# Recurrent gates in row halves of the array, and the first layer's mixing weights split by a converting DMA

## The chip, the cores and the metric

One core of a Trainium2 chip runs the whole program. The metric is the device time of one execution in microseconds (us), compared by the median of several runs. The engines are TensorE (PE, with its weight loads PEld), VectorE (DVE), ScalarE (ACT), GpSimd (POOL) and SyncE (SP, which only issues DMAs).

## The reference, cut to what matters

An encoder of two layers on 512 tokens of 1024 channels, float32. Each layer is a mixing part (half of it attention in a window, half a recurrence in both directions) and a gated MLP with a convolution. The change touches the recurrence: 512 channels in 8 blocks of 64; per direction two gates, each a 64x64 matrix per block.

```python
def rg_lru(x, w_gate, b_gate, lam, reverse):
    xb = x.reshape(bsz, s, N_LRU_BLOCKS, LRU_BLOCK)
    g = jnp.einsum("bsnc,gncd->gbsnd", xb, w_gate).reshape(2, bsz, s, D_LRU)
    g = g + b_gate[:, None, None, :]
    r_gate = jax.nn.sigmoid(g[0]); i_gate = jax.nn.sigmoid(g[1])
    log_a = -LRU_C * r_gate * jax.nn.softplus(-lam)
    a = jnp.exp(log_a)
    u = jnp.sqrt(-jnp.expm1(2.0 * log_a)) * (i_gate * x)
    return linear_scan(a, u, reverse)
...
rec = (rec_f + rec_b) * jax.nn.gelu(gate, approximate=True)
```

## The kernel before, in words

Activations lie channels by tokens, in tiles of 128 partitions x 512 tokens. To reach float32 accuracy each operand of a big product is split in two float32r parts, a leading one (hi) and a trailing one (lo = value - hi), and each product is three TensorE products (`mm3`, L234 to L237: hi x hi, hi x lo, lo x hi).

Weights come in an order fixed by `weight_plan` (L57), in blocks of up to 1024 columns. `chunk` (L223) hands out the next block and keeps the preparation ahead: `load_to` (L162) issues the load on SP's queue into one of 2 `raw` buffers (L177), `split_to` (L182) lets ScalarE copy to `hi` (L197) and VectorE subtract to `lo` (L198), with 4 buffers each. The second layer's mixing blocks are split during the first layer's MLP by `split_later` (L204), kept in DRAM, and loaded back ready (L172).

The order of the mixing part is written out by hand in `MIX` (L44): q, k, v and g are the four column products of the input projection, in halves a and b of 12 products each; c the convolution of a recurrence tile; t0 to t3 the gates of a tile of 128 channels; S, T and P the scores, transposes and products of a head; u turns the values and copies them into `edge` on GpSimd (L603); e multiplies the recurrence by its gate branch (L624). Between these, a planner puts each engine's instructions in an order of its own, by priority and estimated times, and that order is fixed: every engine and every queue then works in order.

`lru_gates` (L521) runs twice per tile: t_a for the forward, t_b for the backward direction. Each call makes two gates of 128x128 weights, in which the two 64x64 blocks stand on the diagonal and the rest is zero; six products of 512 columns. ScalarE takes tanh from the PSUM bank (L535) and makes the decay, VectorE the input term (L542, L543, L549), then one scan per direction (L552, L555) and the sum of both into `fb` (L557). The products' banks come from a pool of three, `ps_mm` (L124).

## Time and profile before

| what | us |
|---|---|
| median of 3 runs | 1210.29 (1209.95 to 1210.47) |
| the profiled execution's own time | 1209.74 |
| span of the profiled execution | 1208.0 |

The profile is of one execution. The span goes from its first to its last instruction; busy times are of that span. A matmul record covers the whole passage through the array, so records overlap, and the distance from one start to the next is what a product costs in a stream. An arrow in a wait leads to what ended it.

### The profile page before, as it was taken

How to read it: one execution, taken by the hardware profiler on the slowest of the kernel's cores; microseconds unless marked ns; L12 is line 12 of the kernel's file. 1: busy time of each engine (PE TensorE's matmuls, PEld its weight loads, DVE VectorE, ACT ScalarE, POOL GpSimd, SP SyncE). 2: the span in 40 equal slices, each digit the busy share in tenths (PEclk: the TensorE clock that was granted, in tenths of full speed). 3: DMA queues.
4: the chain of work that ended last, by engine and by line, in shares of the span. 5: the costliest groups of instructions: out<-in, count | busy, mean ns of one | idle time of the engine just before them, and what ended most of it. 6: DMA issues, size and time to landing. Idle time of an engine off the chain costs nothing.

```text
span 1208.0 us, 14574 instructions
## 1 busy us (share of the span) xinstructions
PE 1192.5 (99%) x5566; PEld 996.3 (82%) x5566; DVE 757.0 (63%) x1237; ACT 502.3 (42%) x741; POOL 95.1 (8%) x166
## 2 busy tenths in 40 slices
PE   9999999999999999999999999999999999999996
PEld 8878888888888888888888888888888888888886
DVE  7899867866634567653728868486555345565353
ACT  6777744434321334332406778353233212333220
POOL 1010010123210123200000000000000000000000
PEclk9999999999999999999999999999999999999998
DMA  7222213367652467633255542233233232323222
GB/s 239 69 87 86 90 41 123 123 223 247 214 168 90 151 218 243 210 117 105 88 174 164 164 141 71 65 111 102 90 102 95 97 104 88 105 87 105 92 66 70
DMA packets 51061, 151.85 MB, mean 126 GB/s; under 512 B 6448, under 2 KB 9648, under 8 KB 50992
## 3 DMA queue, kind: packets, MB, share of 16 engines
q1 hardware_dynamic: 42208, 122.61, 31.3%
q0 software_dynamic: 8640, 28.32, 7.2%
q8 instruction: 43, 0.70, 0.3%
q14 instruction: 26, 0.21, 0.1%
q10 hardware_dynamic: 144, 0.00, 0.0%
HBM read 129.93 MB, written 20.97 MB: 125 GB/s over the span
## 4 chain that ended last, share of the span: by engine, by line
PE 94%; DVE 4%; issue 1%; POOL 0%; DMA 0%; ACT 0%; POOLq 0%; DVEq 0%; SPq 0%; ACTq 0%
PE dn L237 7%; PE dn L235 7%; PE dn L236 7%; PE pl L237 7%; PE pa L237 7%; PE pa L235 7%; PE pl L235 7%; PE pl L236 7%; PE pa L236 7%; PE out L237 2%; PE out L235 2%; PE out L236 2%; PE xr L235 1%; PE up L235 1%; PE vps L237 1%; PE vps L235 1%
## 5 line engine op out<-in xcount | busy, mean ns | idle before, releaser
L197 ACT ACTIVATE hi<-raw 128x1024 fp32r<-128x1024 f32 (+1 forms) x189 | 197.5, 1046 | 399.3 <-PE dn L236 160.5
L198 DVE TENSOR_TENSOR lo<-raw,hi 128x1024 fp32r<-128x1024 f32 (+1 forms) x189 | 228.0, 1206 | 133.5 <-ACT hi L197 132.4
L805 DVE TENSOR_TENSOR ua<-pa,g_ffn_rb 128x512 f32<-128x512 f32 x44 | 30.4, 692 | 113.7 <-PE pa L237 113.7
L813 ACT ACTIVATE uc<-uc,cols 128x512 f32<-128x512 f32 x48 | 34.8, 725 | 117.4 <-DVE uc L811 117.4
L814 DVE TENSOR_TENSOR uc<-pl,uc 128x512 f32<-128x512 f32 x44 | 30.3, 689 | 44.7 <-PE pl L237 43.9
L782 DVE TENSOR_TENSOR dns<-dn,g_ffn_rb 128x512 f32<-128x512 f32 x30 | 20.5, 689 | 29.4 <-PE dn L237 29.4
L811 DVE SCALAR_TENSOR_TENSOR uc<-ua,cols,uc 128x511 f32<-128x511 f32 x48 | 36.0, 750 | 1.5
L809 DVE SCALAR_TENSOR_TENSOR uc<-ua,cols,uc 128x511 f32<-128x511 f32 x48 | 35.8, 745 | 0.1
L220 POOL DMA_DIRECT2D kept<-lhi x36 | 19.6, 544 | 177.3 <-ACT lhi L214 175.3
L215 DVE TENSOR_TENSOR llo<-lraw,lhi 128x512 fp32r<-128x512 f32 x36 | 24.7, 688 | 10.7 <-ACT lhi L214 10.7
L453 POOL TENSOR_TENSOR fin_r<-fin_ms,expo 128x2 f32<-128x2 f32 x2 | 1.4, 697 | 377.7 <-DVE fin_ms L451 377.7
L669 ACT ACTIVATE prob<-prob,mx 128x192 f32<-128x192 f32 (+1 forms) x64 | 27.4, 430 | 1.1 <-DVE mx L667 0.9
L603 POOL CAST edge<-vh 64x384 fp32r<-64x384 f32 x16 | 8.9, 558 | 236.4 <-ACT vh L598 235.9
L235 PE MATMUL out<-atth,hi 128*128 128x512 f32 x64 | 25.6, 401 | 0.0
L237 PE MATMUL out<-atth,lo 128*128 128x512 f32 x64 | 25.3, 395 | 0.0
L236 PE MATMUL out<-attl,hi 128*128 128x512 f32 x64 | 25.2, 393 | 0.0
L808 DVE TENSOR_SCALAR uc<-ua,cols 128x512 f32<-128x512 f32 x48 | 23.4, 488 | 1.6
L220 POOL DMA_DIRECT2D kept<-llo x36 | 19.6, 544 | 50.5 <-DVE llo L215 47.7
L214 ACT ACTIVATE lhi<-lraw 128x512 fp32r<-128x512 f32 x36 | 22.1, 616 | 0.0
L654 PEld LDWEIGHTS s<-k,q_pair 128*128 128x128 f32 x128 | 20.8, 190 | 1.2
L654 PE MATMUL s<-k,q_pair 128*128 128x192 f32 (+1 forms) x128 | 21.7, 313 | 0.0
L783 DVE TENSOR_TENSOR x<-x,dns 128x512 f32<-128x512 f32 x30 | 20.1, 688 | 0.4
(931 smaller groups left out, 3616.0 us busy)
## 6 DMA issues: line engine op xcount, KB each, us to landing
raw<-in_w SPq DMA_DIRECT2D x183, 512.0 KB, 3.5
lraw<-in_w POOLq DMA_DIRECT2D x36, 256.0 KB, 4.4
kept<-lhi POOLq DMA_DIRECT2D x36, 256.0 KB, 2.5
kept<-llo POOLq DMA_DIRECT2D x36, 256.0 KB, 3.0
hi<-kept SPq DMA_DIRECT2D x36, 256.0 KB, 2.9
lo<-kept SPq DMA_DIRECT2D x36, 256.0 KB, 4.2
x<-in_x SPq DMA_DIRECT2D x8, 256.0 KB, 5.3
out_y<-out SPq DMA_DIRECT2D x8, 256.0 KB, 2.3
```

The lines of the kernel that those rows point to most:

```text
L197: nc.scalar.activation(hi[:, sl], raw[:, sl], AF.Copy)
L198: nc.vector.tensor_tensor(out=lo[:, sl], in0=raw[:, sl], in1=f32(hi[:, sl]), op=ALU.subtract)
L220: nc.gpsimd.dma_start(d, f32(parts[h][n]))
L235: nc.tensor.matmul(ps, a[0], b[0], start=start, stop=False)
L236: nc.tensor.matmul(ps, a[0], b[1], start=False, stop=False)
L237: nc.tensor.matmul(ps, a[1], b[0], start=False, stop=stop)
L654: nc.tensor.matmul(ps[:, o:o + ROWS * w], q_pair[:, b], kt[:, kc0 // 8:(kc0 + w) // 8], start=True, stop=True)
L805: nc.vector.tensor_tensor(out=ua, in0=pa, in1=rbf[0], op=ALU.mult)
L809: nc.vector.scalar_tensor_tensor(out=c[:, 1:], in0=ua[:, :T - 1], scalar=w[0], in1=c[:, 1:], op0=ALU.mult, op1=ALU.add)
L811: nc.vector.scalar_tensor_tensor(out=c[:, :T - 1], in0=ua[:, 1:], scalar=w[2], in1=c[:, :T - 1], op0=ALU.mult, op1=ALU.add)
L813: nc.scalar.activation(c, c, AF.Gelu_apprx_tanh, bias=col("conv_ffn_b", j, l))
L814: nc.vector.tensor_tensor(out=c, in0=pl_, in1=c, op=ALU.mult)
```

## The change

The gates of both directions of a tile now stand in one 128x128 block per gate: block row half s holds, in its columns, the forward matrix of sub-block s in the same half and the backward one in the other half. A product of one half of the rows (64 partitions in, 128 out) gives both directions of one sub-block. So a call makes one gate for both directions: three products for each row half, each half in a PSUM bank of its own. The first call (t_a) makes the decay gate of both directions, the second (t_b) the input gate, the root and the scans. The backward direction then has its two halves of 64 channels in swapped places: `xc_sw`, a copy of the convolved tile with halves swapped, is made by two DMAs on GpSimd's queue, and the backward scan is put onto `fb` by two DMAs that swap back and add. ScalarE's tanh works on 64 partitions at a time. A gate block has 256 columns in place of 512.

In the first layer's mixing part the blocks q, k, v, g and the gates, 20 in all, get `hi` by a DMA on GpSimd's queue that converts float32 to float32r as it writes, and `raw` by a second load on SP's queue; VectorE subtracts. A load of these goes at most three blocks ahead of the one in use, a subtraction two. The host lays out gate weights, biases and decays to match.

```diff
@@ weight_plan
-                plan.append(("gate", l, [(int(step[1]), dg) for dg in range(4)]))
+                plan.append(("gate", l, [(int(step[1]), g) for g in range(2)]))
@@ encoder
+    def segments(i):
+        return [slice(a, min(a + 512, width(i))) for a in range(0, width(i), 512)]
...
-    def is_kept(i):
-        w, l, bs = plan[i]
-        return l == 1 and (w == "gate" or w == "w_in" and bs[0][1] != 12)
+    def by_dma(i):
+        w, _, bs = plan[i]
+        return w == "gate" or w == "w_in" and bs[0][1] != 12
@@ load_to
-            if is_kept(i):
+            if by_dma(i):
                 if i > state["use"] + 3:
                     return
                 highs[i] = p_hi.tile([P, 1024], F32R, tag="hi", name=f"hi{i}")
...
+                if i in kept:
+                    lows[i] = p_lo.tile([P, 1024], F32R, tag="lo", name=f"lo{i}")
+                    for n, t in enumerate((highs[i], lows[i])):
+                        for h, sl in enumerate(segments(i)):
+                            nc.sync.dma_start(f32(t[:, sl]), kept[i][n, h])
+                else:
+                    ws = slice(0, width(i))
+                    nc.gpsimd.dma_start(highs[i][:, ws], w_d[i][:, ws])
+                    raws[i] = p_raw.tile([P, 1024], F32, tag="raw", name=f"raw{i}")
+                    nc.sync.dma_start(raws[i][:, ws], w_d[i][:, ws])
@@ split_to
-            if is_kept(i) and i > state["use"] + 2:
+            if by_dma(i) and i > state["use"] + 2:
                 return
...
+            if i in highs:
+                hi = highs.pop(i)
+                lo = p_lo.tile([P, 1024], F32R, tag="lo", name=f"lo{i}")
+                ws = slice(0, width(i))
+                nc.vector.tensor_tensor(out=lo[:, ws], in0=raws.pop(i)[:, ws], in1=f32(hi[:, ws]), op=ALU.subtract)
+                halves[i] = (hi, lo)
+                state["split"] += 1
+                continue
...
-    later = [i for i in range(len(plan)) if is_kept(i)]
+    later = [i for i in range(len(plan)) if by_dma(i) and plan[i][1] == 1]
@@ convolve
             xcs[t] = plain_split(p_h, "h", c, f"xcs{l}_{t}")
+            xc_sw[t] = big(p_h, "h", f"xsw{l}_{t}")
+            swapped(xc_sw[t], c)
@@ layer
+        rows_of = (slice(0, 64), slice(64, P))
+        def swapped(dst, src, **kw):
+            for n in range(2):
+                nc.gpsimd.dma_start(dst[rows_of[n]], src[rows_of[1 - n]], **kw)
@@ lru_gates (new)
+            def products(g, out):
+                ps = [psum(ps_o if n and g and not o_ps[0] else ps_mm, f"gp{l}{t}{g}{n}") for n in range(2)]
+                w = blk(gate["c"], g)
+                for a, b in ((0, 0), (0, 1), (1, 0)):
+                    for n, rows in enumerate(rows_of):
+                        nc.tensor.matmul(ps[n], w[a][rows], xcs[t][b][rows], start=a + b == 0, stop=a == 1)
+                for n in range(2):
+                    for d in range(2):
+                        i = ((l * 2 + d) * 2 + g) * 4 + t
+                        rows = rows_of[n ^ d]
+                        with urgent():
+                            nc.scalar.activation(out[d][rows], ps[n][rows], AF.Tanh, scale=0.5, bias=half_b[rows, i:i + 1])
...
+            if 0 in gs:
+                products(0, ws)
...
+            if 1 in gs:
+                ti = [big(p_t, "t", f"ti{l}{t}{d}") for d in range(2)]
+                products(1, ti)
+                nc.scalar.activation(both, both, AF.Sqrt, scale=0.25)
+                for d, (a, w, u) in enumerate(zip(gate["a"], ws, ti)):
+                    nc.vector.scalar_tensor_tensor(out=u, in0=u, scalar=1.0, in1=xc_sw[t] if d else xc[t],
+                                                   op0=ALU.add, op1=ALU.mult)
+                    nc.vector.tensor_tensor(out=u, in0=u, in1=w, op=ALU.mult)
...
+                        nc.vector.tensor_tensor_scan(out=w[:, ::-1], data0=a[:, ::-1], data1=u[:, ::-1], initial=0.0,
                                                      op0=ALU.mult, op1=ALU.add)
-                    nc.vector.tensor_tensor(out=fb[t], in0=fb[t], in1=w, op=ALU.add)
+                        swapped(fb[t], w, accum_op=ALU.add)
@@ lay_out
-                gate[:, :, 2 * d + g, 64 * s:64 * s + 64, 64 * s:64 * s + 64] = a["lru_w"][:, d, g, s::2]
+            o = 64 * (s ^ d)
+            gate[:, :, :, 64 * s:64 * s + 64, o:o + 64] = a["lru_w"][:, d, :, s::2].transpose(0, 2, 1, 3, 4)
```

## Rows read from the trace of the kernel before

**Rows 1.** the page, part 1: busy time, share of the span, instructions

```profile
PE 1192.5 (99%) x5566; PEld 996.3 (82%) x5566; DVE 757.0 (63%) x1237; ACT 502.3 (42%) x741; POOL 95.1 (8%) x166
...
core 0: 1208.0 us, clock 0.996
```

**Rows 2.** busy time by stage; TensorE, weight loads, VectorE, ScalarE, GpSimd, clock, DMA share, GB/s

```profile
0.00:37.00 37.00, 35.95 (x163) 30.50 (x164) 29.98 (x64) 21.45 (x31) 5.31 (x17) 1.00 0.62 209
37.00:170.00 133.00, 130.80 (x671) 110.39 (x670) 115.61 (x251) 101.28 (x181) 10.80 (x16) 1.00 0.26 81
70.00:102.00 32.00, 31.88 (x167) 27.18 (x166) 29.52 (x66) 25.81 (x46) 2.43 (x4) 1.00 0.25 80
636.00:763.00 127.00, 126.16 (x654) 107.38 (x653) 98.74 (x234) 87.17 (x163) 9.70 (x16) 1.00 0.42 133
```

**Rows 3.** timeline of TensorE, first gate call: start us, duration us, operation

```profile
36.93 0.39 PE L235 MATMUL gp<-xcs_0h,hi 128*128 128x512 f32 x1
37.15 0.39 PE L236 MATMUL gp<-xcs_0l,hi 128*128 128x512 f32 x1
...
38.29 0.39 PE L235 MATMUL kps<-xg_g_mix_4h,hi 128*128 128x512 f32 x1
```

**Rows 4.** the tile gp: duration ns min/median/max of weight loads and products

```profile
L235 PEld LDWEIGHTS gp<-xcs_0h,hi x8: 187/188/188, 36.7 to 636.1; 128*128 128x128 f32 x8
L235 PE MATMUL gp<-xcs_0h,hi x8: 389/389/389, 36.9 to 636.3; 128*128 128x512 f32 x8
```

**Rows 5.** timeline of TensorE, attention products of 128 columns

```profile
75.05 0.22 PE L235 MATMUL o<-pt,edge 128*128 128x128 f32 x1
75.11 0.28 PE L236 MATMUL o<-pt,edge 128*128 128x128 f32 x1
```

**Rows 6.** timeline of TensorE, from the scores back to f32r products

```profile
50.16 0.48 PE L235 MATMUL gate<-xg_g_mix_0h,hi 128*128 128x512 f32 x1
50.48 0.40 PE L236 MATMUL gate<-xg_g_mix_0l,hi 128*128 128x512 f32 x1
```

**Rows 7.** groups of ScalarE by shape, 30 to 170 us: busy us, mean ns

```profile
L197 ACT ACTIVATE hi<-raw 128x1024 fp32r<-128x1024 f32 x17 | 17.9, 1051 | 9.6 <-DMA raw<-in_w 6.1 <-PE gate L236 3.5
...
L535 ACT ACTIVATE w<-gp,half_b 128x512 f32<-128x512 f32 x8 | 5.4, 677 | 9.5 <-PE gp L237 9.5
...
L197 ACT ACTIVATE hi<-raw 128x512 fp32r<-128x512 f32 x3 | 1.9, 617 | 0.0
```

**Rows 8.** groups of VectorE by shape, 30 to 170 us

```profile
L198 DVE TENSOR_TENSOR lo<-raw,hi 128x1024 fp32r<-128x1024 f32 x18 | 22.3, 1238 | 2.2 <-ACT hi L197 1.9
...
L567 DVE TENSOR_TENSOR q_pair<-qps,g_mix_rb 64x512 f32<-64x512 f32 x8 | 5.5, 687 | 0.5 <-PE qps L237 0.4
...
L557 DVE TENSOR_TENSOR fb<-fb,w 128x512 f32<-128x512 f32 x4 | 2.7, 686 | 0.1
```

**Rows 9.** groups of GpSimd, the whole span

```profile
L211 POOL DMA_DIRECT2D lraw<-in_w x36 | 20.0, 558 | 1.2 <-DVE h_11l L352 1.2
```

**Rows 10.** DMA issues: KB each, median us to landing

```profile
raw<-in_w SPq DMA_DIRECT2D x183, 512.0 KB, 3.5
lraw<-in_w POOLq DMA_DIRECT2D x36, 256.0 KB, 4.4
```

**Rows 11.** waits, 37 to 170 us: us in total, times, longest

```profile
ACT hi L197 <- DMA raw<-in_w: 6.1, 3, 3.1
...
PE o L237 <- POOL edge L603: 1.0, 2, 0.5
```

**Rows 12.** timeline of VectorE, end of the scans of gate tile 2

```profile
120.01 1.20 DVE L555 TENSOR_TENSOR_SCAN w<-a,ti 128x512 f32<-128x512 f32 x1
121.24 0.69 DVE L557 TENSOR_TENSOR fb<-fb,w 128x512 f32<-128x512 f32 x1
...
127.94 0.68 DVE L624 TENSOR_TENSOR fb<-fb,z 128x512 f32<-128x512 f32 x1
```

**Rows 13.** timeline of GpSimd, the same stretch

```profile
122.61 1.12 POOL L603 CAST edge<-vh 64x384 fp32r<-64x384 f32 x2 [27.74 <-ACT vh L598]
```

More of the change, by code (lines that the diff above doesn't have):

```diff
@@ L151, in pieces @@
     def pieces(i):
[L152 removed]
+        return (slice(0, 1024),) if i else (slice(0, 512), slice(512, 1024))
     def width(i):
         return P * len(plan[i][2])
[L157 to L160 removed]
+    def segments(i):
[3 more added lines that the diff above has]
+        return w == "gate" or w == "w_in" and bs[0][1] != 12
     def load_to(n):
@@ L168, in load_to @@
                 highs[i] = p_hi.tile([P, 1024], F32R, tag="hi", name=f"hi{i}")
-                lows[i] = p_lo.tile([P, 1024], F32R, tag="lo", name=f"lo{i}")
-                for n, t in enumerate((highs[i], lows[i])):
-                    for h in range(width(i) // 512):
-                        nc.sync.dma_start(f32(t[:, 512 * h:512 * h + 512]), kept[i][n, h])
+                if i in kept:
[8 more added lines that the diff above has]
+                    nc.sync.dma_start(raws[i][:, ws], w_d[i][:, ws])
                 state["load"] += 1
@@ L208, in split_later @@
         parts = []
-        for h in range(width(i) // 512):
-            raw = p_t.tile([P, 512], F32, tag="t", name=f"lraw{i}{h}")
-            nc.gpsimd.dma_start(raw, w_d[i][:, 512 * h:512 * h + 512])
-            hi = p_fb.tile([P, 512], F32R, tag="fb", name=f"lhi{i}{h}")
-            lo = p_fb.tile([P, 512], F32R, tag="fb", name=f"llo{i}{h}")
+        for h, sl in enumerate(segments(i)):
+            n = sl.stop - sl.start
+            raw = p_t.tile([P, n], F32, tag="t", name=f"lraw{i}{h}")
+            nc.gpsimd.dma_start(raw, w_d[i][:, sl])
+            hi = p_fb.tile([P, n], F32R, tag="fb", name=f"lhi{i}{h}")
+            lo = p_fb.tile([P, n], F32R, tag="fb", name=f"llo{i}{h}")
             nc.scalar.activation(hi, raw, AF.Copy)
@@ L217, in split_later @@
         for n in range(2):
-            for h in range(width(i) // 512):
-                d = p_kept.tile([P, 512], F32, tag=f"kept{i}{n}{h}", name=f"kept{i}{n}{h}")
+            for h, sl in enumerate(segments(i)):
+                d = p_kept.tile([P, sl.stop - sl.start], F32, tag=f"kept{i}{n}{h}", name=f"kept{i}{n}{h}")
                 nc.gpsimd.dma_start(d, f32(parts[h][n]))
@@ L497, in layer @@
             prepare_decay()
-        xr, xc, xcs = [], [None] * 4, [None] * 4
+        xr, xc, xcs, xc_sw = [], [None] * 4, [None] * 4, [None] * 4
         for t in range(4):
@@ L513, in convolve @@
             xcs[t] = plain_split(p_h, "h", c, f"xcs{l}_{t}")
+            xc_sw[t] = big(p_h, "h", f"xsw{l}_{t}")
+            swapped(xc_sw[t], c)
         fb = [None] * 4
[L518 removed]
+        gate = {}
         o_ps, att_t = [None], [None]
[L521 to L557 removed]
@@ L885, in lay_out @@
         blocks[n] = w.reshape(L, w.shape[1] // P, P, w.shape[2] // P, P).transpose(0, 1, 3, 2, 4)
-    gate = np.zeros((L, 4, 4, P, P), np.float32)
+    gate = np.empty((L, 4, 2, P, P), np.float32)
     for s in range(2):
         for d in range(2):
-            for g in range(2):
-                gate[:, :, 2 * d + g, 64 * s:64 * s + 64, 64 * s:64 * s + 64] = a["lru_w"][:, d, g, s::2]
+            o = 64 * (s ^ d)
+            gate[:, :, :, 64 * s:64 * s + 64, o:o + 64] = a["lru_w"][:, d, :, s::2].transpose(0, 2, 1, 3, 4)
     blocks["gate"] = gate
@@ L907, in lay_out @@
             put(COLS[n, l], a[n][l])
-    for n in ("lru_b", "lru_lam", "g_final"):
-        put(COLS[n], a[n])
+    lru = {}
+    for n in ("lru_b", "lru_lam"):
+        v = a[n].reshape(L, 2, -1, 2, 64).copy()
+        v[:, 1] = v[:, 1, :, ::-1]
+        lru[n] = v
+    for n, v in (("lru_b", lru["lru_b"]), ("lru_lam", lru["lru_lam"]), ("g_final", a["g_final"])):
+        put(COLS[n], v)
     rel = a["rel_bias"]
```

58 lines of the change are left out of this document (20 added, 38 removed).

## The prediction

> **What bounds the kernel now.** I read the busy times first: TensorE is busy 1192.5 of the 1208.0 us of the span, at a granted clock of 0.996, which is the 2.4 GHz level [rows 1]. So the end is set by TensorE's stream of products, and an edit counts only as far as it takes time from that stream or opens a hole in it. Then the table by stage, for the two stretches in which the gates are computed. In the first layer's mixing TensorE is busy 130.80 of 133 us, VectorE 115.61, ScalarE 101.28, GpSimd 10.80; in the second layer's 126.16 of 127, 98.74, 87.17 and 9.70 [rows 2]. The holes are 2.2 and 0.8 us. In one full turn of the first layer (70 to 102 us) VectorE is busy 29.52 of 32: it follows close behind TensorE, and is the engine that would stop it next.
>
> The profiled execution took 1209.74 us, 1.74 around the span; the median of the runs is 1210.29, so 0.55 is added to a sum made on the trace. A measurement of this kernel tells about 0.2% (2.4 us) from no change.
>
> **Part 1: the gate products in row halves.** Six products of one call run from 36.93 to 38.29 us, so 0.227 us each, end to start [rows 3]. There are 12 in each of 4 tiles and 2 layers, 96, so 21.8 us of TensorE. After it there are again 96 products and 96 weight loads, of 64 rows each, in 48 pairs whose halves use different rows of the array and different PSUM banks. If a pair runs side by side it takes 0.227 us, the whole 48 x 0.227 = 10.9, and 10.9 us leave the stream. If the halves run one after the other, nothing leaves it.
>
> Do the loads of weights allow a pair? A load lasts 0.187 us [rows 4], but a product of 128 columns starts at 75.05 and the next, with weights of its own, at 75.11 [rows 5]: loads follow each other every 0.06 us, and two of them fit into 0.227. I take the pair at 0.227.
>
> What a change between 128 and 64 rows costs no row shows. It happens on entering and on leaving each of 16 calls, 32 times. Lower bound 0, since between products of one kind there is no gap. Upper bound: the engine empties each time, which is how far a product's record outlasts the start of its successor, 0.389 - 0.227 = 0.162 [rows 3, 4], plus 0.06 at the end of each call for the half that started a load later: 32 x 0.162 + 16 x 0.06 = 6.2. The nearest row is the switch from the f32 scores to f32r products, where the first product takes 50.48 - 50.16 = 0.32 in place of 0.227, 0.09 more [rows 6]. I take 32 x 0.09 = 2.9, since that is also a change of how the array works.
>
> Part 1 on TensorE: -10.9 + 2.9 = -8.0.
>
> **The evacuation.** Tanh over a tile becomes two half tiles of 64 partitions. VectorE's 64x512 operation takes 0.687, like its 128x512 ones [rows 8], so a half costs ScalarE what a whole did, 0.677 [rows 7] (lower bound half of it). That is 4 more per tile, +2.7 us, 10.8 per layer. In the second layer ScalarE goes to 98 of about 123 us, a share of 0.80, where the first layer now has 0.76: cover enough. The banks: a call's two banks are both free after four halves, 2.7 us, in place of 1.4; between the two calls of a tile stand 12 key products, 12 x 0.227 = 2.7. That just fits; were it gone, each second call would wait up to 1.3 us.
>
> **Part 2: the first layer's mixing weights.** 16 blocks of 1024 columns and 4 of the gates lose their ScalarE pass: 16 x 1.051 + 4 x 0.617 = 19.3 us [rows 7], more than the 10.8 that the halves add. This is off the path; I count it at nothing. VectorE keeps its subtraction, 1.238 each [rows 8]; the gates' falls from 512 to 256 columns, worth 0 to 0.34 each. VectorE also loses the four additions of the two scans per layer, 4 x 0.686 = 2.7 [rows 8]. Per turn VectorE falls by about 1.0 from 29.5 and TensorE by about 1.0 from 32: it stays as close behind as it was.
>
> GpSimd's queue gets 20 converting loads and, in two layers, 32 copies of half tiles. An issue takes 0.558 [rows 9], so 36 in the first layer are 20 us beside its 10.80 of 133: hidden. What can stand behind one are the edge copies, for which TensorE already waits 1.0 us in that stretch [rows 11]. In the turn shown the second scan ends at 121.21; two adding copies issue until 122.3; the next edge copies start at 122.61 [rows 12, 13]. They fit by 0.3. The adding copies must land before the multiplication by the gate branch at 127.94 [rows 12]; at the 4.4 us of the slowest comparable load [rows 10] they land at 126.7. Hidden by 1.2 us; if it slips, VectorE stands there and everything behind it.
>
> SP's queue keeps 20 loads, of the same blocks; the bytes double for these 20, some 8.5 MB over 133 us, at a DMA share that stands at 0.26 [rows 2]: hidden. At the start, where the share is 0.62, one converting load of 0.5 MB at 209 GB/s could push the others by 2.5 us; TensorE had no hole there beyond its first microsecond [rows 2], and I take 0 of 0 to 2.5.
>
> What can't be read is how long a converting load takes. Lower bound: a plain load of such a block, 3.5 us; from above the GpSimd load of half the size, 4.4, and twice that, 8.8 [rows 10]. A block's tile comes free, and the load goes, four uses ahead; the subtraction stands two uses ahead, so between them one block's products, 24 x 0.227 = 5.4 us, and less around a gate block. I take 5 us, near the GpSimd load, and the wait as mostly covered.
>
> **The sum.** -8.0 from the gates. Holes: TensorE comes to each wait about 1 us earlier while what it waits for is about as late, so the 3.0 us of holes may grow; ScalarE's relief pulls the other way. Bounds -3.0 and +3.0, I take +0.5. Together -7.5: 1209.74 - 7.5 = 1202.2, and 1202.8 against the median.
>
> **The rivals.**
> *The halves don't overlap* (the change does not do what it says). Each half product then takes its own 0.227, 96 of them, the 2.9 of mode changes come on top, and the kernel is at 1213. For it: the trace has no product of fewer than 128 rows. Against it: weights and products already overlap freely. It decides from the point at which a pair takes over 0.39 us.
> *The engine empties at each change.* Then the upper bound of 6.2 holds in place of 2.9: -10.9 + 6.2 + 0.5 = -4.2, 1206.1. For it: between unlike products the rows do show lost time [rows 6]. Against it: those rows lose half as much. The Trainium skill (TensorEngine Tiling (Array Packing), Key Properties) says that changing the tiling mode drains the engine; no run here shows it yet.
> *The weight loads bind.* If a pair must wait for two loads end to end, 2 x 0.187 = 0.374, a pair saves 0.454 - 0.374 = 0.08, 3.8 in all, 2.9 of it eaten: 1209.4. Against it stand the loads at 0.06. The Trainium skill (TensorE: Matmul & The Clock Gate, Part 3) has loads overlap running products only when the row groups differ; the trace does not agree, since loads of all rows run beside products of all rows here at 0.227.
> *VectorE stands at the conversion.* Its queue is in order, and the subtraction now waits for two loads. Before, ScalarE stood for the raw load three times, 6.1 us in all, 2.0 each [rows 11], with time to spare. VectorE has 133 - 115.6 = 17 us free in that stretch; 20 waits use it up from 0.85 us each. At 2.0 each, 40 - 17 = 23 us come through: 1226, slower. For it: a landing that is unknown, a queue that is 0.92 full in the turn. Against it: the lead above. A milder form, in which TensorE gets 3 to 7 us of holes, gives 1206 to 1210.
>
> **How the numbers follow.** Overlapping halves and covered loads 0.52 (1198.4 to 1206; the lower end is -10.9 with 1 us of the holes gone); the engine empties 0.12; the milder stand of VectorE 0.12, half of it beyond 1207.9; loads bind 0.08; no overlap 0.09; VectorE stands in full 0.07. So faster by over 0.2% (under 1207.9) 0.52 + 0.12 + 0.06 = 0.70; within 0.06 + 0.08 = 0.14; slower (over 1212.7) 0.09 + 0.07 = 0.16. The range from 1198 to 1211 holds the first four, 0.84.
>
> **What would show it.** Right: gate products whose second half starts some 0.06 us after the first and pairs 0.227 apart, so 5 us fewer in each layer's mixing; the first product after a call late by about 0.09; ScalarE's share in the first layer down by some 8 us; GpSimd's share up by 20; holes of TensorE near 3 us. Wrong: halves 0.227 apart; the subtractions or the gate branch's multiplication waiting on DMA for more than 17 us in all; TensorE waiting for edge copies or for ScalarE's halves for more than 3 us.

## The result, and the profile after

The changed kernel takes 1218.28 us (median, 1215.70 to 1219.41, 4 runs) against 1210.12 beside it: a ratio of 1.0066, 95% interval 1.0054 to 1.0077. It is **slower by 8.2 us**, where 1202.8 was forecast and the range ended at 1211. The profiled execution took 1215.70, 2.6 under the median.

The page, part 1, the span, and the busy time by stage, each stage taken from the same work as in [rows 2] (columns as there):

```profile
PE 1193.5 (98%) x5566; PEld 989.1 (81%) x5566; DVE 747.1 (62%) x1229; ACT 503.6 (41%) x753; POOL 126.9 (10%) x218
...
core 0: 1213.9 us, clock 0.994
...
38.00:174.00 136.00, 130.32 (x669) 106.37 (x668) 109.49 (x247) 98.82 (x182) 28.15 (x45) 0.99 0.49 143
640.00:771.00 131.00, 126.18 (x653) 104.27 (x650) 96.14 (x231) 97.19 (x179) 19.25 (x30) 0.99 0.46 137
```

TensorE does not set the time alone any more: it stands for 5.7 us of the first stretch and 4.8 of the second, against 2.2 and 0.8 before. It is as busy as before although the calls save 2.3 us in each, since products under a lower clock take longer (below). ScalarE has lost only 2.5 us in the first layer, where the prediction named some 8: four wide conversions of other weights stand in the same stretch and stayed. In the second layer it has gained 10.

**The products are faster, by less than forecast.** Timeline of TensorE around the first gate call, which answers to [rows 3] ("x2" is a pair):

```profile
37.48 0.39 PE L255 MATMUL kps<-xg_g_mix_3h,lo 128*128 128x512 f32 x1
37.80 0.50 PE L562 MATMUL gp<-xcs_0h,hi 64*128 64x512 f32 x2
38.14 0.40 PE L562 MATMUL gp<-xcs_0l,hi 64*128 64x512 f32 x2
38.37 0.40 PE L562 MATMUL gp<-xcs_0h,lo 64*128 64x512 f32 x2
38.70 0.50 PE L253 MATMUL kps<-xg_g_mix_4h,hi 128*128 128x512 f32 x1
39.04 0.40 PE L254 MATMUL kps<-xg_g_mix_4l,hi 128*128 128x512 f32 x1
```

The halves of a pair start together and run side by side: three pairs take 0.90 us, six products took 1.36. But the first step into the call and the one behind it take 0.32 and 0.34, and inside it only the middle pair takes 0.23. From the last product before the call to the second one after it 1.56 us pass, before it was 8 x 0.227 = 1.82. Of the 16 calls, ten save 0.26 like this one and six, which come after a 128-column product, 0.34: 10 x 0.26 + 6 x 0.34 = 4.6 us in all, not 8.0.

**The two long holes.** In both layers the first product that reads `vl` comes late. VectorE, GpSimd's queue and TensorE in the first layer:

```profile
64.49 1.23 DVE L205 TENSOR_TENSOR lo<-raw,hi 128x1024 fp32r<-128x1024 f32 x1 [1.82 <-DMA hi<-in_w]
65.63 0.69 DVE L370 TENSOR_TENSOR xcs_1l<-xc,xcs_1h 128x512 fp32r<-128x512 f32 x1
66.23 0.68 DVE L637 TENSOR_TENSOR vl<-vtp,vh 128x512 fp32r<-128x512 f32 x1
...
57.94 1.73 POOL L545 DMA_DIRECT2D fb<-w  x2 [7.82 <-ACT pt L733]
59.32 0.95 POOL L179 DMA_DIRECT2D hi<-in_w  x1
...
66.97 0.39 PE L255 MATMUL o<-pt,vl 128*128 128x256 f32 x1 [2.63 <-DVE vl L637]
```

The subtraction waits for a converting load; the load was issued behind two adding DMAs on the same queue; `vl` stands behind the subtraction, and TensorE waits 2.63 us for `vl`. The second layer:

```profile
662.63 0.69 DVE L662 TENSOR_TENSOR fb<-fb,z 128x512 f32<-128x512 f32 x1 [3.04 <-DMA fb<-w]
663.25 0.69 DVE L370 TENSOR_TENSOR xcs_1l<-xc,xcs_1h 128x512 fp32r<-128x512 f32 x1
663.85 0.68 DVE L637 TENSOR_TENSOR vl<-vtp,vh 128x512 fp32r<-128x512 f32 x1
...
664.58 0.39 PE L255 MATMUL o<-pt,vl 128*128 128x256 f32 x1 [2.51 <-DVE vl L637]
```

Here it is the multiplication by the gate branch that waits, for the adding DMA. In the kernel before, the same two products start without a wait:

```profile
66.35 0.30 PE L237 MATMUL o<-pt,vl 128*128 128x256 f32 x1
...
657.37 0.39 PE L237 MATMUL o<-pt,vl 128*128 128x256 f32 x1
```

Behind each hole TensorE's products of 512 columns come 0.43 us apart instead of 0.227 for a while:

```profile
69.89 0.63 PE L255 MATMUL kps<-xg_g_mix_0h,lo 128*128 128x512 f32 x1
70.32 0.63 PE L253 MATMUL kps<-xg_g_mix_1h,hi 128*128 128x512 f32 x1
...
68.50:71.70 3.20, 3.20 (x12) 2.62 (x10) 3.14 (x7) 0.49 (x1) 0.59 (x2) 0.50 0.74 197
```

The last line is the table by stage for that stretch: the granted clock is 0.50, the 1.2 GHz level; TensorE had stood 2.63 us and then worked for 1.5 us at 1.00 before it fell. Seven products from 68.89 to 71.99 take 3.10 where 7 x 0.227 = 1.59 would do, so this hole costs 1.5 us more than its length.

The waits of VectorE behind this (37 to 176 and 632 to 772 us), the DMAs' landing, and ScalarE's halves (30 to 174 us), which answer to [rows 11], [rows 10] and [rows 7]:

```profile
DVE lo L205 <- DMA hi<-in_w: 15.1, 7, 3.2
...
DVE fb L662 <- DMA fb<-w: 4.6, 2, 3.0
...
hi<-in_w POOLq DMA_DIRECT2D x16, 512.0 KB, 4.6
...
fb<-w POOLq DMA_DIRECT2D x16, 128.0 KB, 4.4
...
L568 ACT ACTIVATE w<-gp,half_b 64x512 f32<-64x512 f32 x16 | 10.5, 680 | 11.8 <-PE gp L562 8.7 <-issue 3.0
L568 ACT ACTIVATE ti<-gp,half_b 64x512 f32<-64x512 f32 x16 | 10.4, 676 | 0.2
```

A tanh over 64 partitions costs 0.68, what one over 128 costs in [rows 7].

### The profile page after: what moved, and what is told of

It reads as the page before. It is cut to its first block, busy times and chain, and to the rows that moved or that the text cites. A ratio compares the mean times of both kernels' runs of the same rounds, so it can differ in the third digit from the quotient of the medians.

```text
span 1213.9 us, 14718 instructions
## 1 busy us (share of the span) xinstructions
PE 1193.5 (98%) x5566; PEld 989.1 (81%) x5566; DVE 747.1 (62%) x1229; ACT 503.6 (41%) x753; POOL 126.9 (10%) x218
## 4 chain that ended last, share of the span: by engine, by line
PE 86%; ACT 5%; issue 3%; DVE 3%; DMA 2%; POOL 0%; POOLq 0%; DVEq 0%; ACTq 0%
PE dn L253 7%; PE dn L255 7%; PE dn L254 7%; PE pa L253 7%; PE pl L253 7%; PE pl L255 7%; PE pa L255 7%; PE pl L254 7%; PE pa L254 7%; PE out L255 2%; PE out L253 2%; PE out L254 2%; PE xr L253 1%; DMA hi<-in_w 1%; PE up L253 1%
## 5 line engine op out<-in xcount | busy, mean ns | idle before, releaser
L214 ACT ACTIVATE hi<-raw 128x1024 fp32r<-128x1024 f32 (+1 forms) x169 | 178.2, 1055 | 386.0 <-PE dn L254 160.6
L205 DVE TENSOR_TENSOR lo<-raw,hi 128x1024 fp32r<-128x1024 f32 (+1 forms) x20 | 21.2, 1059 | 16.6 <-DMA hi<-in_w 15.1
L568 ACT ACTIVATE w<-gp,half_b 64x512 f32<-64x512 f32 x32 | 21.0, 680 | 24.7 <-PE gp L562 15.2
L233 DVE TENSOR_TENSOR llo<-lraw,lhi 128x512 fp32r<-128x512 f32 (+1 forms) x36 | 23.6, 659 | 10.6 <-ACT lhi L232 10.5
L545 POOL DMA_DIRECT2D fb<-w x16 | 14.2, 1008 | 143.9 <-ACT prob L707 63.7
L232 ACT ACTIVATE lhi<-lraw 128x512 fp32r<-128x512 f32 (+1 forms) x36 | 21.3, 593 | 2.8 <-DMA lraw<-in_w 2.8
```

The source lines that it names most:

```text
L214: nc.scalar.activation(hi[:, sl], raw[:, sl], AF.Copy)
```

## The experiments

All times are medians beside runs of the kernel before on the same chip (1209.84 to 1210.12). A turn is the work on one tile in `MIX`, from its first gate product to that of the next tile, the last one to the end of the mixing. The shifts are read from each trace: the start of the same product of TensorE minus its start in the kernel before, where these stand at 69.91 (first gate product of the second turn), 170.75 (first `stats` product, the end of the mixing), 662.77 and 763.31 (the same two in the second layer).

| kernel | us | ratio, 95% interval | layer 1, turn 2 | its end | layer 2, turn 2 | its end |
|---|---|---|---|---|---|---|
| after | 1218.28 | 1.0054 to 1.0077 | +3.3 | +4.2 | +8.8 | +8.2 |
| gates_only | 1210.57 | 1.0000 to 1.0018 | -0.6 | +0.1 | +3.5 | +2.6 |
| dma_only | 1212.77 | 1.0016 to 1.0036 | +1.4 | +3.5 | +3.5 | +3.5 |
| full_rows | 1218.08 | 1.0054 to 1.0081 | +5.9 | +7.7 | +11.3 | +12.0 |
| noswap | 1221.79 | 1.0080 to 1.0108 | +0.9 | +6.8 | +7.9 | +11.8 |
| half_tanh | 1224.70 | 1.0101 to 1.0132 | +1.5 | +9.1 | +11.9 | +13.7 |
| after_u | 1210.17 | 0.9990 to 1.0008 | -0.1 | +2.1 | +1.5 | +2.6 |
| gates_only_u | 1210.60 | 0.9995 to 1.0014 | -0.7 | +3.2 | +2.6 | +1.9 |
| no_hi_wait | 1212.54 | 1.0009 to 1.0028 | +0.7 | +0.5 | +4.7 | +5.6 |
| before_u | 1207.85 | 0.9974 to 0.9993 | -1.9 | -0.6 | -1.4 | -1.7 |
| after_no_add | 1211.69 | 1.0006 to 1.0025 | +0.9 | +4.7 | +4.7 | +3.9 |
| after_u_sq | 1214.95 | 1.0024 to 1.0050 | +3.4 | +6.1 | +5.4 | +7.8 |
| gates_u_sq | 1214.33 | 1.0025 to 1.0051 | -1.6 | +3.0 | +2.4 | +7.2 |
| whole_tanh | 1209.26 | 0.9982 to 1.0000 | -0.5 | +3.6 | +2.7 | +0.5 |
| whole_tanh_u | 1209.51 | 0.9982 to 1.0001 | -0.4 | +3.8 | +4.8 | +2.6 |
| by_half_u | 1216.28 | 1.0036 to 1.0066 | +0.7 | +6.0 | +7.0 | +8.4 |
| by_half_gu | 1220.60 | 1.0069 to 1.0100 | +0.3 | +10.1 | +10.7 | +12.1 |
| whole_nohi | 1200.50 | 0.9906 to 0.9939 | -1.0 | -3.5 | -3.9 | -6.2 |
| whole_gates | 1200.89 | 0.9912 to 0.9941 | -1.7 | -4.3 | -4.7 | -7.0 |

### The parts alone

*gates_only*: part 1 without part 2. The first layer's mixing weights are split by ScalarE and VectorE as before.

```diff
-        w, _, bs = plan[i]
-        return w == "gate" or w == "w_in" and bs[0][1] != 12
+        w, l, bs = plan[i]
+        return l == 1 and (w == "gate" or w == "w_in" and bs[0][1] != 12)
...
```

> The change without its second part: the first layer's mixing weights are split by ScalarE and VectorE as before, the gates stay in row halves with the halves swapped by DMA. Theory 1 (the holes come from VectorE standing for DMAs: the converting load in the first layer, the adding copies in the second): the first layer's hole of 2.6 us and the slow clock behind it go, unless the adding copies take its place there, and the second layer's stays: 1213 to 1215. Theory 2 (twice as many evacuations on ScalarE make everything behind them late, whatever the DMAs): ScalarE has 19 us more in the first layer than in the changed kernel, so 1218 to 1224.

*dma_only*: part 2 on the kernel before, the hunks of `load_to` and `split_to` alone.

```diff
-    def is_kept(i):
+    def by_dma(i):
...
```

> The kernel before with the second part alone: gates in four full products, the first layer's mixing weights with leading halves by converting DMA. Theory 1: VectorE stands for converting loads, some 15 us in the first layer as in the changed kernel, TensorE loses 3 to 5 us: 1213 to 1215. Theory 2: ScalarE is relieved of 19 us and nothing is lost: 1208 to 1210.

*full_rows*: the changed kernel with every gate product over all 128 rows, so that a gate is the sum over both blocks.

```diff
-                        nc.tensor.matmul(ps[n], w[a][rows], xcs[t][b][rows], start=a + b == 0, stop=a == 1)
+                        nc.tensor.matmul(ps[n], w[a], xcs[t][b], start=a + b == 0, stop=a == 1)
```

> The changed kernel, but every gate product uses all 128 rows, so the two products of a pair run one after the other; the gates are then sums over both sub-blocks, which is not what the reference computes, and the rest is as it was. If halves run side by side as the trace reads (0.90 us a call in place of 1.36), 16 calls lose 0.46 each: 1218.3 + 7.4 = 1225.7, less what the later start of the waits gives back (theory 1: up to 3, so 1222 to 1226). If the halves bring nothing, 1218.

*noswap*: gates_only, but ScalarE's tanh writes the other half of the partitions for the backward direction, so the swapping DMAs go and VectorE adds the scans again.

```diff
-                            nc.scalar.activation(out[d][rows], ps[n][rows], AF.Tanh, scale=0.5, bias=half_b[rows, i:i + 1])
+                            nc.scalar.activation(out[d][rows], ps[n][rows_of[n ^ d]], AF.Tanh, scale=0.5,
+                                                 bias=half_b[rows, i:i + 1])
...
-                        swapped(fb[t], w, accum_op=ALU.add)
+                        nc.vector.tensor_tensor(out=fb[t], in0=fb[t], in1=w, op=ALU.add)
...
```

> Gates in row halves, first layer's weights as before, and no swapping DMA: ScalarE's tanh reads one half of the partitions of a bank and writes the other half of the tile, so that both directions lie in place; VectorE adds the scans as before. Theory 1: no VectorE wait on a new DMA is left, the row halves bring 16 x 0.46 = 7.4 us, with up to 2 us given back: 1203 to 1205. Theory 2: the doubled evacuation is still there, so the holes are: 1210 to 1216.

The sum is not additive: the parts alone cost 0.7 and 2.9 us, together 8.2. All three kernels have a shorter end of the span, worth 2.0 to 2.5 us (see the last section); without it they cost some 2.7, 5.4 and 10.6, so the gap is 2.5 us and not 4.6, and neither part is as cheap as it looks. gates_only lies below both ranges, dma_only just under theory 1's, with 7.2 us of waits for converting loads where 15 were expected. full_rows came out at 1218.08, where 1222 to 1226 was expected if the halves run side by side. They do: its first call takes 1.81 us by the measure by which the changed kernel's takes 1.56. But by its median it is no slower than the changed kernel (the profiled executions, from which the shifts come, are the slowest of its runs and the fastest of the other's), so TensorE's saving is worth nothing there: it only comes earlier to its waits. And noswap, which has none of the new DMAs, is the slowest of the four and outside both ranges. So DMAs are not the whole cause. What noswap shares with the change is ScalarE's doubled tanh.

### The doubled tanh

*half_tanh*: the kernel before with its tanh in two halves.

```diff
-                    with urgent():
-                        nc.scalar.activation(o, ps, AF.Tanh, scale=0.5, bias=half_b[:, i:i + 1])
+                    for rows in (slice(0, 64), slice(64, P)):
+                        with urgent():
+                            nc.scalar.activation(o[rows], ps[rows], AF.Tanh, scale=0.5, bias=half_b[rows, i:i + 1])
```

> The kernel before, with each tanh over a gate's bank made as two instructions of 64 partitions; nothing else. Theory 1 (ScalarE has no slack in the last turn of a layer, so its doubled evacuation makes the softmax and the transposed probabilities late): ScalarE busy some 10.8 us more per layer, TensorE with new holes of 1 to 4 us per layer, most of them in the last turn, in front of products that read pt; 1212 to 1217. Theory 2 (only waits for DMAs cost the change its gain, ScalarE's share of 0.8 is cover enough): 1209.5 to 1210.8, no new hole over 0.5 us.

It costs 14.6 us, more than both theories gave, and not where theory 1 had most of it: the last turns are only 1.4 us longer in each layer. The first layer's other turns lose 1.0, 2.0 and 4.2 us, the second layer's 2.9, 0.4 and 0.0. ScalarE, VectorE and TensorE in the third turn of the first layer, and below them the same in the kernel before:

```profile
125.42 1.06 ACT L548 ACTIVATE w<-w 128x1024 f32<-128x1024 f32 x1
...
128.32 1.22 DVE L553 TENSOR_TENSOR_SCAN fb<-a,ti 128x512 f32<-128x512 f32 x1
...
133.16 0.68 DVE L697 TENSOR_TENSOR pt<-ptw,pt 128x512 fp32r<-128x512 f32 x1
...
133.88 0.39 PE L236 MATMUL o<-pt,vh 128*128 128x256 f32 x1 [1.11 <-DVE pt L697]
```

```profile
116.10 1.06 ACT L547 ACTIVATE w<-w 128x1024 f32<-128x1024 f32 x1
...
118.87 1.22 DVE L552 TENSOR_TENSOR_SCAN fb<-a,ti 128x512 f32<-128x512 f32 x1
...
126.21 0.68 DVE L696 TENSOR_TENSOR pt<-ptw,pt 128x512 fp32r<-128x512 f32 x1
```

The turn begins 3.5 us later than before, the square root (`w<-w`) and the scan behind it come 9 us later: the halves make ScalarE late, and the planner has put the root with its two table loads in the middle of a head's exponentials. VectorE then does the scans close in front of `pt`, for which TensorE waits. In the last turn `pt` itself comes late from ScalarE; in the kernel before it did not, and ScalarE was the one that waited (half_tanh, then the kernel before):

```profile
166.82 0.39 PE L235 MATMUL o<-pt,vh 128*128 128x256 f32 x1 [1.04 <-ACT pt L696]
```

```profile
156.07 0.60 ACT L695 ACTIVATE pt<-ptw 128x512 fp32r<-128x512 f32 x1 [0.86 <-PE ptw L686]
```

So a share of 0.76 over the layer hid how little is free inside a turn. From a tile's first decay pass (`a<-w,spn`) to the first `pt` behind its root, some 18 us, ScalarE in the kernel before stood idle for 2.2, 0.8, 0.1 and 0.95 us in the first layer's four turns and for 3.7, 3.0, 2.8 and 0.95 in the second's. The halves add 4 x 0.68 = 2.7 us per turn. The two turns that lose least, 0.4 and 0.0, had 3.0 and 2.8 free. The second layer's first turn does not fit: it had 3.7 and still loses 2.9, with a hole of 0.69 us in front of a product that reads `vh` and a granted clock of 0.66 from 668 to 672 us. How much of the loss is the halves' own time and how much the order that the planner then chose was not separated.

### The two waits for DMAs

*after_u*: the changed kernel with `u0` moved 12 products earlier in the hand-written order, which puts `vl` ahead of both waiting instructions in VectorE's queue. *gates_only_u* is the same on gates_only, *before_u* on the kernel before, as a control.

```diff
-MIX = ("q0 c0 k0a t0a k0b t0b v0a S0 v0b S1 g0a c1 u0 g0b T0 q1a q1b P0 T1 c2 k1a t1a k1b P1 t1b "
+MIX = ("q0 c0 k0a t0a k0b t0b v0a S0 v0b S1 u0 g0a c1 g0b T0 q1a q1b P0 T1 c2 k1a t1a k1b P1 t1b "
```

> The changed kernel, with the step u0 of the hand-written order moved 12 products earlier (behind S1 in place of behind c1), so that VectorE's vl of the first tile stands ahead of the subtraction and of the gate branch's multiplication that wait for DMAs. Theory 1 (the time is lost where VectorE stands for a DMA with something behind it that TensorE needs at once; the two holes of 2.6 and 2.5 us in front of vl, and about 1.5 us of lower clock behind each, are the larger part): 1209 to 1212. Theory 2 (VectorE's 15 us of standing bind the whole stretch, wherever vl is): under 3 us gained, 1215 to 1218.

> Part 1 alone (1210.6 before this), with u0 moved as in the run above. Theory 1 (turn 0 of the second layer costs 3.9 us because the multiplication stands for the adding DMA ahead of vl): that loss goes, 1206 to 1208; what is left of the missing 8 us is in the last turns, on ScalarE. Theory 2 (the adding DMA hides, ScalarE's doubled tanh is the whole loss): 1209.5 to 1211.

> Control: the kernel before with u0 moved 12 products earlier, as in after_u. Theory 1 (after_u gained 8 us because vl no longer stands behind waits for DMAs, which the kernel before does not have): no gain here, 1209.5 to 1211. Rival (an earlier u0 is a gain of its own, whatever the change does): 1203 to 1207.

*no_hi_wait*: VectorE's subtraction no longer reads the converted tile.

```diff
-                nc.vector.tensor_tensor(out=lo[:, ws], in0=raws.pop(i)[:, ws], in1=f32(hi[:, ws]), op=ALU.subtract)
+                nc.vector.tensor_tensor(out=lo[:, ws], in0=raws[i][:, ws], in1=raws.pop(i)[:, ws], op=ALU.subtract)
```

> The changed kernel, with the trailing halves of the first layer's 20 blocks computed from the plain load alone (raw minus raw, so zero): VectorE waits for the plain load and no longer for the converting one; every load, subtraction and product is still there. Theory 1 (VectorE standing 15 us for the converting loads costs the first layer its gain): TensorE is some 3 to 5 us earlier at the end of the first layer's mixing, the second layer loses its 4 us as before, 1213 to 1215.5. Theory 2 (the converting loads hide, order and ScalarE cost the time): 1217 to 1219.

*after_no_add*: the changed kernel without the adding DMAs.

```diff
-                        swapped(fb[t], w, accum_op=ALU.add)
```

> The changed kernel without the two DMAs per tile that add the backward scan onto fb (so the backward direction is left out of the recurrence); VectorE's order is the same, its multiplication by the gate branch just no longer waits for a DMA. Theory 1 (turn 0 of the second layer loses 5.1 us because that multiplication stands for the adding DMA ahead of vl): the second layer's shift stays at about +4 instead of going to +8, 1213 to 1215. Rival (the hole of that turn is ScalarE's or VectorE's own lateness, and the DMA only the last of several): under 2 us gained, 1216.5 to 1218.5.

after_u is 8.1 us faster than the changed kernel, as theory 1 had it: the shift at the second turn of each layer goes from +3.3 and +8.8 to -0.1 and +1.5. The control gains 2.1 us (0.9974 to 0.9993), between the ranges of its two theories; so 2.1 come with an earlier `u0` anyway, and if the two add up, some 6 belong to the change. In gates_only_u the move brings nothing by the median: the second layer's first turn is 4.0 us shorter than in gates_only, as theory 1 had it, but the second turn of the first layer is 3.6 longer, where TensorE now waits for `xcs` and `k` from VectorE (0.56 and 1.47 us). The time lies in theory 2's range, but because a gain and a loss cancel, and not because the adding DMA hides.

no_hi_wait gives back 5.7 us, most of it in the first layer (+4.2 to +0.5 at its end), a little more than theory 1's 1213 to 1215.5. after_no_add gives back 6.6 by the medians, where theory 1 had 3 to 5, and 4.3 by the shifts at the second layer's end (the changed kernel's profiled execution is its fastest). As theory 1 had it, these come in the second layer's first turn, which now adds nothing, so that the shift stays at +4.7. The first layer's second turn starts at +0.9 instead of +3.3, but that is lost again by the layer's end (+4.7 against +4.2). GpSimd's queue and VectorE in after_no_add, at the place of the first hole:

```profile
56.45 0.56 POOL L179 DMA_DIRECT2D hi<-in_w  x1 [6.62 <-PE gate L255]
...
63.31 1.21 DVE L205 TENSOR_TENSOR lo<-raw,hi 128x1024 fp32r<-128x1024 f32 x1
```

Without the adding DMAs the converting load goes at 56.45 in place of 59.32, and the subtraction finds it there. So the two parts meet on GpSimd's queue. But this is only part of VectorE's standing: without the adding DMAs it still waits 13.6 us for converting loads in that layer, against 15.1.

### ScalarE relieved

*after_u_sq* and *gates_u_sq*: after_u and gates_only_u with the decay's squares on GpSimd.

```diff
-                    nc.scalar.activation(a2, a, AF.Square)
+                    nc.gpsimd.tensor_tensor(out=a2, in0=a, in1=a, op=ALU.mult)
```

> after_u (1210.2 before this) with the eight squares per layer of the decay (a2) on GpSimd in place of ScalarE, some 5 us of ScalarE per layer. Theory 1 (what after_u still lacks is lost on ScalarE, above all in the last turns, where the square root's two table loads now stand in the middle of a head's exponentials): ScalarE some 5 us lower per stretch, the last turns 2 us shorter, 1205 to 1208.5. Rival (VectorE's standing for the converting loads is what is left, or GpSimd's squares slow VectorE by as much): 1209.5 to 1213.

> gates_only_u (1210.6 before this, part 1 alone with u0 earlier) with the same squares on GpSimd. Theory 1: ScalarE, which has its 19 us of weight conversions here, gets back 5 of the 10.8 us that the halves add: 1206 to 1209, and no faster than after_u_sq by more than 1. Rival: no change against gates_only_u, 1209.5 to 1212.

Both are slower, by 4.8 and 3.7 us than without. after_u_sq, groups of GpSimd over the span and of VectorE from 37 to 176 us, and behind them VectorE's group of L711 in after_u:

```profile
L578 POOL TENSOR_TENSOR a<-a 128x512 f32<-128x512 f32 x16 | 18.5, 1158 | 51.8 <-ACT a L575 33.8 <-PE o L255 10.2 <-PE gp L562 7.7
...
L579 DVE SCALAR_TENSOR_TENSOR w<-a,w 128x512 f32<-128x512 f32 x8 | 5.5, 686 | 2.9 <-POOL a L578 2.9
L711 DVE TENSOR_SCALAR prob<-prob,sm 128x192 f32<-128x192 f32 x24 | 8.1, 392 | 0.0
```

```profile
L711 DVE TENSOR_SCALAR prob<-prob,sm 128x192 f32<-128x192 f32 x24 | 6.7, 336 | 0.0
```

A square takes GpSimd 1.16 us. VectorE waits 2.9 us for them, where it waited 3.8 for ScalarE's, so that is not the loss; but its own scaling takes 392 ns in place of 336, and from 37 to 176 us it is busy for 117.6 in place of 111.5. Both times lie above the rivals' ranges too; after_u_sq's rival had the direction, that the squares would slow VectorE. This was no clean test of ScalarE, so the next one takes the doubling itself away.

*whole_tanh* and *whole_tanh_u*: the changed kernel and after_u with one tanh per bank.

```diff
-                for n in range(2):
-                    for d in range(2):
-                        i = ((l * 2 + d) * 2 + g) * 4 + t
-                        rows = rows_of[n ^ d]
-                        with urgent():
-                            nc.scalar.activation(out[d][rows], ps[n][rows], AF.Tanh, scale=0.5, bias=half_b[rows, i:i + 1])
+                for n in range(2):
+                    i = ((l * 2 + n) * 2 + g) * 4 + t
+                    with urgent():
+                        nc.scalar.activation(out[n], ps[n], AF.Tanh, scale=0.5, bias=half_b[:, i:i + 1])
```

> The changed kernel, u0 where it was, with each of a call's two banks taken by one tanh over 128 partitions in place of two over 64 (so the two directions' halves stay mixed and the recurrence is not the reference's; sizes and counts of everything behind are the same). ScalarE has 10.8 us less per layer. Theory 1 (the doubled evacuation is a loss of its own beside the waits for DMAs): the last turns and the turns of the first layer lose 4 to 8 us less in all, 1210 to 1214; the hole in front of vl in the second layer stays. Rival (with the waits for DMAs there, ScalarE's 10.8 us are covered): under 2 us gained, 1216 to 1218.5.

> after_u (1210.2) with the same whole tanh, so without the doubled evacuation and without the waits in front of vl; the recurrence is left mixed as in the run above. Theory 1: TensorE's 7.4 us come through against the control with the earlier u0 (1207.9), but for the first layer's standing for converting loads: 1201 to 1205. Rival (VectorE's standing and the lower clock behind holes take the rest, whatever ScalarE does): 1207 to 1210.

whole_tanh is 9.0 us faster than the changed kernel, a little more than theory 1's best, and the long hole in front of `vl` is gone in both layers, where theory 1 let the second layer's stay: the backward scan of that turn in the second layer starts at 650.73 in place of 652.78, and VectorE no longer waits for its adding DMA. whole_tanh_u was forecast at 1201 to 1205 and is no faster than whole_tanh; its rival had 1207 to 1210. Most of its loss, 3.7 us, is in the third turn of the first layer (VectorE, then TensorE; the last line is whole_tanh's):

```profile
102.54 1.22 DVE L205 TENSOR_TENSOR lo<-raw,hi 128x1024 fp32r<-128x1024 f32 x1 [2.70 <-DMA hi<-in_w]
...
104.34 1.38 DVE L603 TENSOR_TENSOR q_pair<-qps,g_mix_rb 64x512 f32<-64x512 f32 x2
...
105.87 0.47 PE L562 MATMUL gp<-xcs_2h,hi 64*128 64x512 f32 x1 [2.40 <-DVE q_pair L603]
...
104.48 0.76 PE L562 MATMUL gp<-xcs_2h,hi 64*128 64x512 f32 x1 [2.27 <-DVE q_pair L603]
```

The same wait for a converting load, now with `q_pair` behind it, for which the gates' second bank waits. whole_tanh has this hole too, so it does not come from moving `vl`: with `vl` out of the way or in time, something else that TensorE needs stands behind the subtraction.

*whole_nohi* takes both away in the changed kernel (the edits of whole_tanh and no_hi_wait). *whole_gates* is gates_only with the edit of whole_tanh. Both leave the two directions mixed, and whole_nohi has trailing halves of zero, so they show where the time goes and are no kernels to use.

> whole_tanh and no_hi_wait together in the changed kernel: one tanh over 128 partitions per bank (the recurrence is left mixed), and the trailing halves of the first layer's blocks computed from the plain load alone (so zero). Theory 1 (the doubled evacuation and VectorE's standing for converting loads are, with the hole in front of vl that the first of them brings about, the whole of what is missing): TensorE's 7.4 us come through in both layers, 1202 to 1205. Rival (some of the gain is lost elsewhere, to waits not yet named): 1206 to 1209.5.

> Part 1 alone (no converting load, ScalarE makes the leading halves as before the change) with one tanh over 128 partitions per bank; the recurrence is left mixed. ScalarE then does what it did before the change. Theory 1 (part 2 is needed only to pay for the doubled tanh): TensorE's 7.4 us come through without it, 1202 to 1205.5. Rival (ScalarE's conversions hold the first layer up as soon as TensorE comes earlier): first layer no better than before the change, 1206 to 1209.5.

Both come to some 9 us faster than the kernel before, past the better end of theory 1 (2.5 and 2.1 us of it are at the very end of the span, see the last section). Busy time by stage and the waits of TensorE in both layers' mixing, whole_nohi, then the busy time of whole_gates:

```profile
38.00:164.00 126.00, 125.62 (x664) 103.84 (x663) 110.10 (x246) 87.01 (x164) 30.41 (x45) 1.00 0.54 155
632.00:757.00 125.00, 124.44 (x656) 103.43 (x656) 95.90 (x231) 86.62 (x164) 20.57 (x30) 1.00 0.48 143
...
PE o L255 <- POOL edge L639: 0.4, 1, 0.4
...
PE o L255 <- POOL edge L639: 0.6, 2, 0.3
```

```profile
38.00:164.00 126.00, 124.94 (x657) 103.45 (x658) 108.44 (x244) 99.23 (x180) 20.93 (x30) 1.00 0.33 97
632.00:757.00 125.00, 124.42 (x658) 103.68 (x656) 95.24 (x231) 85.87 (x163) 20.56 (x30) 1.00 0.48 143
```

TensorE is full again, the granted clock is 1.00, and ScalarE in whole_gates is as full as in [rows 2], weight conversions included. So the doubled tanh and VectorE's standing at converting loads are the whole of the loss, and part 2 is not needed to get the gain of part 1. They divide by layer: with the doubling alone taken away (whole_tanh) the first layer still ends at +3.6 and the second then gains 3.1 us; with the converting wait alone taken away (no_hi_wait) the first ends at +0.5 and the second loses 5.1. The adding DMAs stand in both fast kernels, where VectorE waits for them 1.4 and 0.4 us in all; in the changed kernel, whose doubled tanh makes the scan late, it waits 4.6 in the second layer alone.

### A full recurrence without the doubling

*by_half_u* and *by_half_gu*, on after_u and gates_only_u: each bank stays one tile, four copies in place of two put each half of the convolved tile into both halves of a tile of its own, and the scans run on half tiles.

```diff
-                        nc.vector.tensor_tensor_scan(out=fb[t], data0=a, data1=u, initial=0.0,
+                    nc.vector.tensor_tensor_scan(out=fb[t][f], data0=a[f], data1=u[f], initial=0.0,
...
-                        nc.vector.tensor_tensor_scan(out=w[:, ::-1], data0=a[:, ::-1], data1=u[:, ::-1], initial=0.0,
+                    nc.vector.tensor_tensor_scan(out=w[b, ::-1], data0=a[b, ::-1], data1=u[b, ::-1], initial=0.0,
...
```

> A layout that computes the recurrence in full with whole tanh: each bank stays one tile (forward gates of one 64-channel block in one half, backward gates of the same block in the other) through decay, root and input term; the convolved tile is copied to both halves by four DMAs in place of two, and the scans run on half tiles, four per gate tile in place of two. ScalarE 10.8 us less per layer than after_u, VectorE some 4 x 2 x 1.2 = 9.6 more. Theory 1 (ScalarE's evacuation is what after_u lacks): 1203 to 1207.5. Rival (VectorE, 0.8 full, is the next bound): 1209 to 1214.

> The same layout on gates_only_u (1210.6), so without converting loads: ScalarE as full as before the change (it keeps its weight conversions), VectorE some 7 us per layer fuller than before the change. Theory 1: VectorE no longer stands for converting loads, which the first layer of by_half_u does; 1203 to 1207.5. Rival (VectorE is now the fullest engine beside TensorE): 1210 to 1215.

The rival held in both, worse than it had it. Scans of VectorE in by_half_u, 37 to 176 us:

```profile
L591 DVE TENSOR_TENSOR_SCAN fb<-a,ti 64x512 f32<-64x512 f32 x8 | 10.0, 1247 | 0.1
L593 DVE TENSOR_TENSOR_SCAN w<-a,ti 64x512 f32<-64x512 f32 x8 | 9.8, 1230 | 0.1
```

A scan over 64 partitions takes as long as one over 128, so VectorE gets what ScalarE lost. No full recurrence with row halves was found that beats the kernel before; before_u does, by 2.1 us, without the change.

## Why the prediction was wrong

**The step that failed first** is "The evacuation": the halves' size was right (0.68 us each, and ScalarE's busy time rose by 10.0 us in the second layer's stretch), but "cover enough" was read from ScalarE's share of a whole layer. Between a tile's decay and `pt` it had less than 1 us free in three of the first layer's four turns and in the second layer's last, and a turn gets 2.7 more. What stands behind the tanh comes late: on ScalarE the root, the exponentials and `pt`, on VectorE the scans and what is queued behind them. I counted nothing; taking the doubling away is worth 9.0 us in the changed kernel, 9.7 in part 1 alone (1210.57 to 1200.89). In the changed kernel that makes the first turns of the two layers 4.1 and 5.4 us shorter and the last ones 0.9 and 1.6, while the first layer's third turn grows by 3.6, with the hole at `q_pair`.

**Part 2, "the wait as mostly covered".** The landing was right: 5 us assumed, 4.6 measured. The lead was not 5.4 us: VectorE stood 15.1 us in the first layer. One reason is that a load can stand on GpSimd's queue behind adding DMAs that wait for the scan; I had asked what edge copies stand behind those DMAs, not that the other new DMAs do. But 13.6 us of the wait stay without the adding DMAs, and 7.2 with part 2 alone, so the lead was too short by itself. The 15.1 us lie within the 17 us free, and still they cost 5.7, because the position of the wait counts and not only its sum: behind it stood `vl` or `q_pair`. So this rival, given 0.07 in full and priced at 23 us, had the right mechanism and the wrong arithmetic. ScalarE's relief, the aim of part 2, was worth nothing: whole_tanh, with part 2, is 8.4 us slower than whole_gates without, and no_hi_wait, which has the relief and the doubled tanh without the wait, is 2.0 slower than gates_only.

**The start, "0 of 0 to 2.5".** The first gate product comes 0.9 us later than before in the changed kernel, 1.5 in dma_only and 0.1 in gates_only, so part 2 costs something there as well.

**"Hidden by 1.2 us"**, the adding DMA: 4.4 us landing assumed and measured as median, but in the second layer's first turn, where the kept loads run beside it, one took 7.4 and VectorE waited 3.0, and the doubled tanh had made the scan later. In whole_tanh VectorE waits for it 0.6 us in all, in whole_tanh_u still 2.7 once.

**Part 1 on TensorE, -8.0**: overlap and pair were right, the change of mode was mis-sized. (10.9 - 4.6) / 32 = 0.20 us per change where I took 0.09; the upper bound, the engine emptying each time, was 32 x 0.162 + 16 x 0.06 = 6.1 (6.2 is written there), and 6.3 was measured. So the rival was right about the size of this term. The Trainium skill (TensorEngine Tiling (Array Packing), Key Properties) says that changing the tiling mode drains the engine; the trace agrees, with 0.20 us for each change.

**Holes, +0.5**: in whole_gates TensorE is 7.0 us early at the end of the second mixing, 4.6 of it from the products and 1.4 from holes (3.0 us in the two stretches of [rows 2], 1.6 in those of whole_gates); 1.0 is not accounted for. So without the losses above the sum would have been -7.0, close to the forecast -7.5 but of other parts.

## What to carry to other kernels

Read an engine's slack in the turn and in front of the instruction that someone waits for, not from its share of a stage; an engine with 20% free can have none for eighteen microseconds (ScalarE in the kernel before, 106 to 124 us). When an edit saves time on the bounding engine but adds instructions or waits to queues that feed it, price the place: list what stands behind each new wait in its queue and who reads that next. Two edits that share a queue must be priced together, and a cheap way to tell causes apart is to undo each alone and then all at once.

## What the runs showed of the hardware

- Products of 64 rows in different halves of the array run side by side, but a change between 64 and 128 rows costs TensorE 0.20 us, as the mean of entering and leaving a call: 32 of them take 6.3 of the 10.9 us that 48 pairs save.
- After TensorE had stood for 2.63 us, it worked for 1.5 us at a granted clock of 1.00; then the clock was 0.50 (the 1.2 GHz level) from 68.5 to 71.7 us.
- ScalarE takes 0.68 us for a tanh over 64 or 128 partitions, VectorE 1.2 for a scan over either, GpSimd 1.16 for a square that takes ScalarE 0.62.
- Runs of one kernel scatter by 3.7 us over four of the changed kernel and 4.2 over four of noswap, against 1.2 over ten of before_u. Holes of TensorE alone do not explain it: in gates_u_sq it stands idle about as long as in the changed kernel, and the runs scatter by 1.1 over five.
- In the profiles of the kernels that have new DMAs on GpSimd's queue the span ends 3.2 to 3.7 us after VectorE has computed the last output; in the others (before, before_u, noswap, half_tanh) it takes 5.7 to 6.0. Why was not tried. The gain is no merit of the row halves, since dma_only has it too; it is why the changed kernel's profiled execution is only 6.0 us longer although TensorE is 8.2 late.
